# A convolution with max-pooling: whole copies of the second sum, and column maxima taken from SBUF

## The chip, the core and the metric

The kernel runs on one NeuronCore of a Trainium2 chip. Its engines work side by side, each through its own instructions in order: TensorE (PE in the profile) multiplies matrices into PSUM, VectorE (DVE), ScalarE (ACT) and GpSimd (POOL) do elementwise work, and SyncE (SP) issues DMAs, as ScalarE and GpSimd also may. PSUM has eight banks here, each of 128 partitions by 512 f32 numbers; GpSimd has no operand there in this kernel. The metric is the device time of one execution in microseconds. The median of three runs before the change is 103.07 us (103.0 to 103.2).

## The reference

```python
batch, c_in, h, w, c_out, k = 16, 64, 64, 64, 128, 3
x_pad = np.pad(x, ((0, 0), (0, 0), (pad, pad), (pad, pad)))
conv[b, co] += weight[co, ci, kh, kw] * x_pad[b, ci, kh:kh+h, kw:kw+w]   # over all ci, kh, kw
output[b, c, i, j] = np.max(conv[b, c, 2*i:2*i+2, 2*j:2*j+2])
```

It is a 3 x 3 convolution with padding, from 64 to 128 channels, on 16 images of 64 x 64, followed by the maximum over 2 x 2 blocks. Inputs and output are f32.

## The kernel before, in words

Two images lie in the 128 partitions together (64 channels each), as bf16 tiles `xb`. The output rows of a pair of images are cut into four quarters of 16 rows; there are 32 quarters `s`, and each has two halves `h`, one for each image. The two halves use different 64 rows of TensorE's array, so two chains of matmuls run side by side (`product` pairs them). One step of such a chain ("product") is three matmuls, one for each column of the filter, each of 512 or 504 columns. 512 columns are eight row pairs of 64 columns: one PSUM bank.

Of each pair of rows that is pooled, the kernel does not compute both rows in full. It makes two sums, a first one (bank `ta`) and a second one (bank `tb`), from products on combinations of image rows: `s` (the sum of the two rows), `e` (their difference) and `d` (the difference of rows two apart). In 52 of the 64 cases (type W) the first sum starts with P2 on `e`; `SE` copies it into the second bank as a seed (line L355); P0 adds to the first, P3 to the second; `EV` brings the negated first sum to SBUF (L349); `MX` writes the larger of the second sum and that back into the second bank (L360, VectorE, one input in PSUM and one in SBUF); P1 adds the product on `s`, and the second bank then holds the maximum over the two rows. In the other 12 (type K) the sums come from products straight on `xb` (PA, PB, PR) and `EV` does not negate (L345). The last quarter is worked off in two parts of half the rows; the second part (`s` = 32) keeps its two sums in two banks and has no row maximum.

What is left is the maximum over neighbouring columns. Before the change there are two ways: `OD` lets ScalarE copy the odd columns of the second bank to an SBUF tile `od` (L370, 256 of 512 columns), and `CM` lets VectorE take the maximum of the even columns in PSUM and of `od` (L389); or, where the order says `OD+`, nothing is copied and `CM` is a reduction from PSUM alone (L385). When both halves of a quarter are done, a DMA stores the tile `o` (L396). The part `s` = 32 has a reduction of its own over both banks, rows and columns at once (L378).

The combinations are made in SBUF: `S` on VectorE (L308), `E` on VectorE or, as `E+`, on GpSimd (L308), `D` on GpSimd or, as `D+`, on VectorE (L322); an `&` makes two quarters at once. A GpSimd instruction is told to wait for the VectorE instruction of this kind that stands last before it in the order: such VectorE instructions go through `on_vector`, which remembers them, and GpSimd's through `on_gpsimd`, which adds the wait (L66 to L72). Image loads (`L`) are issued by GpSimd under the same rule, except for the first rows, which SyncE loads as f32 and which are cast by ScalarE and VectorE (X steps).

At the start the weights are combined into blocks (g0, g1, g2, D0, D2, GS, GM, GP), transposed by TensorE (T steps, L146) and copied out of PSUM (V steps, L158 to L164).

The order of all steps is written out in one string, `ORDER`; each engine gets its own instructions in that order. `BANKS` is the list of PSUM banks, taken in turn by each new sum. A `+` sends a step to its other engine (VectorE for `SE+` and `EV+`).

Of the kernel before, what the change touches and what calls it, by code (L numbers as in the profile page):

```python
# [11 lines left out]
def kernel(  # L12
# [9 lines left out]
    nc = tc.nc  # L22
# [26 lines left out]
    o_pool = ctx.enter_context(tc.tile_pool(name="o_pool", bufs=12))  # L49
# [314 lines left out]
    def odd(s, h, alt):  # L364
        if alt:
            direct.add((s, h))
            return
        i0, i1 = span_of(s)
        dst = tile_of(od, od_pool, s, WO, "od")[:, h, i0:i1]
        nc.scalar.copy(out=dst, in_=acc[:, tb[s, h], i0:i1, 1::2])  # L370

    def colmax(s, h, free):
        i0, i1 = span_of(s)
        o = tile_of(ot, o_pool, s, WO, "o")
        t = acc[:, tb[s, h], i0:i1]
        if s == N:
            a, b = sorted((ta[s, h], tb[s, h]))
            nc.vector.tensor_reduce(  # L378
                out=o[:, h, i0:i1],
                in_=acc[:, a : b + 1 : b - a, i0:i1].rearrange("p k r (w two) -> p r w k two", two=2),  # L380
                axis=mybir.AxisListType.XY,
                op=MAX,
            )
        elif (s, h) in direct:
            nc.vector.tensor_reduce(  # L385
                out=o[:, h, i0:i1], in_=t.rearrange("p r (w two) -> p r w two", two=2), axis=mybir.AxisListType.X, op=MAX
            )
        else:
            nc.vector.tensor_tensor(out=o[:, h, i0:i1], in0=t[:, :, 0::2], in1=od[s][:, h, i0:i1], op=MAX)  # L389
        made.setdefault(s, []).append(h)  # L390
        if len(made[s]) < 2:
            return
# [44 lines left out]
    for m in ("G0", "G1", "G2"):  # L437
# [6 lines left out]
    ORDER = """  # L444
        g2+ g1 D2 g0 TG2 TD2 uG1+ XOa+ TG1 VD2+ VG2 D0 XOb+ GS+ XEa XEb+ X2 TD0 L.1.0.17 TG0 VD0 L.1.17.33
        VG0+ F.0.0 GP uGP+ F.2.0 F.0.1 F.3.1 GM F.1.0 S.0 X1+ F.1.1 EV+.0.1 EV.0.0 F.3.0 F.2.1 VG1+ uGM+
        PA1.1.0 PB1.1.0 L.0.49.64 PA2.1.0 MX.0.1 MX.0.0 PB2.1.0 PA1.1.1 PB1.1.1 PR.0.0 X4 PR.0.1 X3 L.1.33.64
        L.2.0.33 S.1 L.2.33.64 OD+.0.1 PA2.1.1 CM.0.1 EV.1.0 PB2.1.1 S.3 PB1.3.1 PA1.3.0 PB1.3.0 MX.1.0
        PA1.3.1 EV.1.1 OD.0.0 L.3.0.64 PA2.3.0 TGM MX.1.1 PR.1.1 PR.1.0 CM.0.0 PB2.3.1 PA2.3.1 S.2 OD.1.1
        PB2.3.0 D+.2 E&.2 CM.1.1 VGM EV.3.0 OD+.1.0 TGP P2.4.1 PA1.5.0 CM.1.0 MX.3.0 PA1.5.1 PB1.5.0 EV.3.1  # L450
        PA2.5.1 PA2.5.0 PR.3.0 SE.4.1 MX.3.1 D.4 VGP+ P0.4.1 PB2.5.0 P2.2.1 S.4 P3.4.1 EV.5.0 P2.4.0 PR.3.1
        S.5 E&.6 S&.7 EV.5.1 EV.4.1 OD.3.0 P2.6.0 SE.2.1 MX.5.0 L.4.0.64 CM.3.0 PR.5.0 SE.4.0 P0.2.1 P3.2.1
        OD.3.1 P0.4.0 P3.4.0 MX.4.1 EV.2.1 D.6 OD+.5.0 EV.4.0 CM.3.1 P2.6.1 PA1.9.0 SE.6.0 SE.6.1 CM.5.0 E+.8
        MX.2.1 MX.4.0 P1.4.1 P0.6.0 OD.4.1 P1.4.0 P1.2.1 P3.6.0 EV.6.0 S&.9 CM.4.1 D+.7 OD.2.1 P0.6.1 EV.6.1
        PB1.5.1 S.10 P3.6.1 P2.7.0 PA2.9.0 CM.2.1 MX.6.0 MX.6.1 P1.6.0 PB2.5.1 P2.7.1 D.10 OD.4.0 SE.7.0
        EV.9.0 MX.5.1 OD.6.0 P1.6.1 P0.7.0 P3.7.0 PR.5.1 P2.8.1 SE.7.1 EV.7.0 CM.4.0 CM.6.0 OD+.6.1 D.8 P2.8.0
        P0.7.1 CM.6.1 P3.7.1 PB1.9.0 MX.7.0 OD.5.1 CM.5.1 P1.7.0 SE.8.0 SE.8.1 E&.10 S.11 D+.11 P0.8.1 EV.7.1
        PB2.9.0 E&+.12 P0.8.0 OD.7.0 P3.8.0 EV.8.1 P2.10.1 P2.2.0 MX.7.1 EV.8.0 L.5.0.64 MX.9.0 PR.9.0 P3.8.1
        CM.7.0 MX.8.0 P1.8.0 P1.7.1 SE.10.1 P0.10.1 OD.7.1 P3.10.1 SE.2.0 P0.2.0 EV.10.1 MX.8.1 P2.11.0 CM.7.1
        P3.2.0 S&.12 P1.8.1 P2.10.0 MX.10.1 OD.8.0 OD.9.0 PA1.9.1 P1.10.1 CM.8.0 CM.9.0 D.14 PA1.15.1 OD.8.1  # L460
        EV.2.0 CM.8.1 SE.11.0 OD.10.1 SE.10.0 MX.2.0 PA2.9.1 P0.11.0 P1.2.0 CM.10.1 P0.10.0 P3.10.0 PB1.9.1
# [36 lines left out]
    BANKS = (
        "0123456710346520137365417346027351426507431270652347105234651370451275302641057631256401723451670312"
        "745632071634025674123706153427601526314"  # L500
# [9 lines left out]
    on_act = [i for i, v in enumerate(ORDER.split()) if v.split(".")[0] in ("EV", "SE", "OD")]  # L510
# [49 lines left out]
```

## Time and profile before

| what | value |
|---|---|
| median of the runs | 103.07 us |
| the profiled execution's own time | 103.78 us |
| its span, first to last instruction | 102.0 us |
| granted TensorE clock, mean | 0.999 |
| busy: PE / DVE / ACT / POOL | 95.7 / 91.2 / 82.3 / 56.7 us |
| L360, row maximum, VectorE, 512 columns | x62, 691 ns |
| L389, column maximum, VectorE, 256 from PSUM and `od` | x49, 415 ns |
| L385, column maximum as a reduction | x13, 682 ns |
| L370, copy of odd columns, ScalarE | x49, 379 ns |
| L355 and L349, whole copies, ScalarE | x50, 584 ns and x49, 603 ns |
| L322, `d` on GpSimd, 1024 columns bf16 | x18, 2129 ns |
| L308 and L322 on VectorE, 1024 columns bf16 | 681 ns |

An instruction's duration in the profile holds a fill and a drain that overlap with its neighbours: in a run of equal instructions they start closer together than they last. "Idle before" is the time an engine stood still ahead of an instruction, with what ended it.

### The profile page before, as it was taken

How to read it: one execution, taken by the hardware profiler on the slowest of the kernel's cores; microseconds unless marked ns; L12 is line 12 of the kernel's file. 1: busy time of each engine (PE TensorE's matmuls, PEld its weight loads, DVE VectorE, ACT ScalarE, POOL GpSimd, SP SyncE). 2: the span in 40 equal slices, each digit the busy share in tenths (PEclk: the TensorE clock that was granted, in tenths of full speed). 3: DMA queues.
4: the chain of work that ended last, by engine and by line, in shares of the span. 5: the costliest groups of instructions: out<-in, count | busy, mean ns of one | idle time of the engine just before them, and what ended most of it. 6: DMA issues, size and time to landing. Idle time of an engine off the chain costs nothing.

```text
span 102.0 us, 2471 instructions
## 1 busy us (share of the span) xinstructions
PE 95.7 (94%) x897; PEld 59.5 (58%) x897; DVE 91.2 (89%) x199; ACT 82.3 (81%) x182; POOL 56.7 (56%) x43
## 2 busy tenths in 40 slices
PE   6989999999999999999999999999999999999900
PEld 2468544565556664444676656776545777677800
DVE  3577999889999999999999989998999999999750
ACT  5467827899889899799967999998989998989410
POOL 2044427194693680953998666569688099930000
PEclk9999999999999999999999999999999999999999
DMA  2988999999999999999894379983260053220352
GB/s 75 263 322 175 162 171 214 225 235 231 228 218 245 327 202 191 240 209 212 143 330 151 116 146 190 202 284 105 70 231 14 16 195 107 103 103 0 135 202 86
DMA packets 11293, 18.04 MB, mean 177 GB/s; under 512 B 784, under 2 KB 9360, under 8 KB 10640
## 3 DMA queue, kind: packets, MB, share of 16 engines
q0 software_dynamic: 1584, 7.59, 40.8%
q1 hardware_dynamic: 9424, 10.16, 29.7%
q10 hardware_dynamic: 272, 0.13, 0.4%
q8 instruction: 7, 0.11, 0.4%
q14 instruction: 6, 0.05, 0.2%
HBM read 17.07 MB, written 8.39 MB: 250 GB/s over the span
## 4 chain that ended last, share of the span: by engine, by line
PE 88%; DMA 5%; DVE 1%; ACT 1%; SPq 0%; issue 0%; DVEq 0%
PE acc L197 88%; DMA kfirst<-in_x_dram 5%; DVE o L378 1%; PE acc L146 1%; ACT wt L162 0%; ACT xb L401 0%; SPq L81 0%; DVEq L555 0%
## 5 line engine op out<-in xcount | busy, mean ns | idle before, releaser
L197 PEld LDWEIGHTS <-wt 64*128 64x128 bf16 x864 | 56.2, 94 | 33.1 <-issue 4.2
L197 PE MATMUL acc<-d,wt 64*128 64x504 bf16 (+3 forms) x312 | 63.4, 373 | 0.0
L322 POOL TENSOR_TENSOR d<-xb 128x1024 bf16<-128x1024 bf16 x18 | 38.1, 2129 | 17.1 <-DVE s L308 9.0
L197 PE MATMUL acc<-s,wt 64*128 64x504 bf16 (+3 forms) x204 | 47.2, 367 | 0.0
L360 DVE TENSOR_TENSOR acc<-acc,ev 128x512 f32<-128x512 f32 (+1 forms) x64 | 42.1, 683 | 1.8 <-ACT od L370 0.4
L197 PE MATMUL acc<-e,wt 64*128 64x512 bf16 (+2 forms) x156 | 38.2, 372 | 0.0
L355 ACT COPY acc<-acc 128x512 f32<-128x512 f32 (+1 forms) x52 | 29.6, 576 | 3.5 <-PE acc L197 2.3
L349 ACT ACTIVATE ev<-acc 128x512 f32<-128x512 f32 (+1 forms) x51 | 29.9, 595 | 2.0 <-PE acc L197 1.3
L197 PE MATMUL acc<-xb,wt 64*128 64x504 bf16 (+6 forms) x192 | 27.2, 333 | 0.5 <-ACT wt L162 0.5
L370 ACT COPY od<-acc 128x256 f32<-128x256 f32 (+1 forms) x51 | 18.6, 374 | 5.2 <-PE acc L197 3.1
L389 DVE TENSOR_TENSOR o<-acc,od 128x256 f32<-128x256 f32 (+1 forms) x51 | 20.2, 410 | 0.9 <-ACT od L370 0.6
L308 POOL TENSOR_TENSOR e<-xb 128x512 bf16<-128x512 bf16 (+1 forms) x8 | 12.2, 1523 | 5.3 <-PE acc L197 2.7
L328 POOL DMA_DIRECT2D xb<-in_x_dram x11 | 6.2, 564 | 10.5 <-DVE xb L403 6.7
L308 DVE TENSOR_TENSOR s<-xb 128x1024 bf16<-128x1024 bf16 (+1 forms) x20 | 11.4, 575 | 0.2 <-ACT xb L401 0.2
L385 DVE TENSOR_REDUCE o<-acc 128x256 f32<-128x512 f32 x13 | 8.9, 682 | 0.2 <-PE acc L197 0.2
L345 ACT COPY ev<-acc 128x512 f32<-128x512 f32 x11 | 6.4, 588 | 0.9 <-PE acc L197 0.6
L308 DVE TENSOR_TENSOR e<-xb 128x1024 bf16<-128x1024 bf16 (+1 forms) x8 | 5.2, 649 | 0.0
L322 DVE TENSOR_TENSOR d<-xb 128x1024 bf16<-128x1024 bf16 (+1 forms) x8 | 5.2, 647 | 0.0
L506 PE MATMUL acc<-const-bfloat16-1.0 128*128 128x512 bf16 x8 | 3.6, 628 | 0.8 <-PEq L541 0.8
L146 PEld LDWEIGHTS <-wq 128*128 128x128 bf16 x25 | 2.2, 132 | 1.7 <-issue 0.8
L146 PE MATMUL acc<-ident,wq 128*128 128x128 bf16 x25 | 2.9, 291 | 0.0
L506 PEld LDWEIGHTS <-const-bfloat16-1.0 128*128 128x128 bf16 x8 | 1.0, 139 | 2.4 <-issue 2.4
(29 smaller groups left out, 18.0 us busy)
## 6 DMA issues: line engine op xcount, KB each, us to landing
out_dram<-o SPq DMA_DIRECT2D x31, 256.0 KB, 3.8
xb<-in_x_dram POOLq DMA_DIRECT2D x5, 1024.0 KB, 11.4
xb<-in_x_dram POOLq DMA_DIRECT2D x2, 496.0 KB, 10.5
xb<-in_x_dram POOLq DMA_DIRECT2D x1, 528.0 KB, 11.1
ksecond<-in_x_dram SPq DMA_DIRECT2D x1, 512.0 KB, 6.4
kthird<-in_x_dram SPq DMA_DIRECT2D x1, 512.0 KB, 7.1
wraw<-in_weight_dram SPq DMA_DIRECT2D x1, 288.0 KB, 2.9
kfirst<-in_x_dram SPq DMA_DIRECT2D x1, 288.0 KB, 4.7
```

Of the source, the lines that this page charges most:

```text
L146: nc.tensor.transpose(tp[:, (j - lo) * CO : (j - lo + 1) * CO], wq[:, j : j + 2, :].rearrange("a b c -> a (b c)"), ident,)
L197: nc.tensor.matmul(acc[:, t, i0:i1, o0:o1], wt[lo : lo + CI, tap_of(m0, kw, h), :], rows(lo, i0, i1, c0, c1), start=start and kw == 1, sto ...
L308: note(engine.tensor_tensor(out=dst, in0=in0, in1=in1, op=op))
L322: engine.tensor_tensor(out=row["d", s][:, 0:n, :], in0=t[:, f + 1 : f + 1 + n, :], in1=t[:, f - 1 : f - 1 + n, :], op=SUB)
L328: inst = on_gpsimd(nc.gpsimd.dma_start(out=xb[p][:, lo + 1 : hi + 1, :], in_=rows_of(p, lo, hi)))
L345: (nc.vector.tensor_copy if alt else nc.scalar.copy)(out=dst, in_=src)
L349: nc.scalar.mul(dst, src, -1.0)
L355: (nc.vector.tensor_copy if alt else nc.scalar.copy)(out=acc[:, t, i0:i1], in_=acc[:, ta[s, h], i0:i1])
L360: nc.vector.tensor_tensor(out=t, in0=t, in1=ev[s][:, h, i0:i1], op=MAX)
L370: nc.scalar.copy(out=dst, in_=acc[:, tb[s, h], i0:i1, 1::2])
L385: nc.vector.tensor_reduce(out=o[:, h, i0:i1], in_=t.rearrange("p r (w two) -> p r w two", two=2), axis=mybir.AxisListType.X, op=MAX)
L389: nc.vector.tensor_tensor(out=o[:, h, i0:i1], in0=t[:, :, 0::2], in1=od[s][:, h, i0:i1], op=MAX)
```

## The change

A new step `ODW` lets ScalarE copy all 512 columns of the second bank to SBUF, into an `od` tile that is twice as wide. `CM` then takes the maximum of the even and the odd columns of that tile: both of VectorE's inputs lie in SBUF. `CM&` does it for both halves of a quarter in one instruction of 512 columns. Counted in the order, 44 of the 64 cases use `ODW` (35 had `OD` before and 9 `OD+`), 17 `OD`, 3 `OD+`; 16 of the 44 go through the eight `CM&`. The pool of `o` tiles shrinks from 12 to 9. The order and the banks are written anew from start to end; among other things eight seeds and one eviction more are VectorE's (`SE+` eight times, `EV+` three times in place of two), five long `d` move from GpSimd to VectorE and four joint `e` the other way, and the transposes TG1 and TGM come before the first product.

```diff
-    o_pool = ctx.enter_context(tc.tile_pool(name="o_pool", bufs=12))
+    o_pool = ctx.enter_context(tc.tile_pool(name="o_pool", bufs=9))
...
-    def odd(s, h, alt):
+    whole = set()
+
+    def odd(s, h, alt, all_columns=False):
+        if all_columns:
+            whole.add((s, h))
+            nc.scalar.copy(out=tile_of(od, od_pool, s, W, "od")[:, h], in_=acc[:, tb[s, h]])
+            return
         if alt:
             direct.add((s, h))
             return
         i0, i1 = span_of(s)
-        dst = tile_of(od, od_pool, s, WO, "od")[:, h, i0:i1]
+        dst = tile_of(od, od_pool, s, W, "od")[:, h, i0:i1, 0:WO]
         nc.scalar.copy(out=dst, in_=acc[:, tb[s, h], i0:i1, 1::2])
 
-    def colmax(s, h, free):
+    def colmax(s, h, joint, free):
         i0, i1 = span_of(s)
         o = tile_of(ot, o_pool, s, WO, "o")
+        if joint:
+            assert {(s, 0), (s, 1)} <= whole
+            nc.vector.tensor_tensor(out=o, in0=od[s][:, :, :, 0::2], in1=od[s][:, :, :, 1::2], op=MAX)
+            store(s, free)
+            return
...
-        else:
-            nc.vector.tensor_tensor(out=o[:, h, i0:i1], in0=t[:, :, 0::2], in1=od[s][:, h, i0:i1], op=MAX)
+        elif (s, h) in whole:
+            t = od[s][:, h]
+            nc.vector.tensor_tensor(out=o[:, h], in0=t[:, :, 0::2], in1=t[:, :, 1::2], op=MAX)
+        else:
+            nc.vector.tensor_tensor(out=o[:, h, i0:i1], in0=t[:, :, 0::2], in1=od[s][:, h, i0:i1, 0:WO], op=MAX)
...
+        GS+ g2 g1 D2 GM TG2 D0 g0 uG1+ uGM+ TD2 L.1.0.17 VD2+ XOa+ XEa+ VG2+ L.1.17.33 XOb+ TG0 TD0 TG1 TGM
+        VG0+ VD0 VGM VG1+ X2 GP F.0.0 XEb L.0.49.64 S.0 X1+ uGP F.2.0 F.1.0 PA1.1.0 L.1.33.64 F.3.0 F.1.1
...
+        P2.19.1 P0.18.0 EV.17.0 S&.24 ODW.18.1 SE+.21.1 P3.18.0 EV.18.0 P2.20.0 CM&.13.1 ODW.16.1 MX.18.0
+        P2.22.0 P0.21.1 D.22 SE.19.1 EV.21.1 P3.21.1 MX.17.0 P0.19.1 P1.18.0 SE.22.0 P3.19.1 P1.17.0 S.23
...
-        CM.31.0 PA2.32.1 PRA.32.0 CM.29.1 P1.31.1 PA2.32.0 CM.32.1 CM.32.0 OD.31.1 CM.31.1
...
+        PB2.32.1 PB2.32.0 CM.30.0 OD.31.0 CM.31.0 MX.31.1 CM.32.1 PRB.32.0 P1.31.1 CM.32.0 OD.31.1 CM.31.1
```

More of the change, by code (lines that the diff above doesn't have):

```diff
@@ L387, in colmax, with store @@
             )
+        elif (s, h) in whole:
+            t = od[s][:, h]
+            nc.vector.tensor_tensor(out=o[:, h], in0=t[:, :, 0::2], in1=t[:, :, 1::2], op=MAX)
         else:
-            nc.vector.tensor_tensor(out=o[:, h, i0:i1], in0=t[:, :, 0::2], in1=od[s][:, h, i0:i1], op=MAX)
+            nc.vector.tensor_tensor(out=o[:, h, i0:i1], in0=t[:, :, 0::2], in1=od[s][:, h, i0:i1, 0:WO], op=MAX)
         made.setdefault(s, []).append(h)
-        if len(made[s]) < 2:
-            return
+        if len(made[s]) == 2:
+            store(s, free)
+    def store(s, free):
+        i0, i1 = span_of(s)
+        o = ot[s]
         p, q = place[quarter(s)]
@@ L444 @@
     ORDER = """
[L445 to L449, printed above, removed]
@@ new lines @@
+        PA2.1.1 OD+.0.0 X3 X4 PB2.1.0 PB2.1.1 PR.0.1 PA1.3.0 PB1.3.0 EV.1.1 EV.1.0 PA1.3.1 OD.0.1 L.2.33.64
+        CM.0.0 PB1.3.1 S.3 MX.1.1 MX.1.0 PR.1.0 CM.0.1 PA2.3.0 PB2.3.0 PA2.3.1 L.3.0.64 PB2.3.1 PR.1.1 EV.3.1
+        ODW.1.0 D+.2 E&.2 EV.3.0 P2.4.1 PA1.5.0 ODW.1.1 S&.4 MX.3.1 D.4 TGP SE.4.1 PR.3.1 PA1.5.1 PA2.5.0 VGP+
+        P0.4.1 EV.5.0 MX.3.0 CM&.1.1 P2.2.1 PR.3.0 OD+.3.1 CM.3.1 PB1.5.0 ODW.3.0 S.5 P2.4.0 E&.7 EV.4.1
+        SE.4.0 PA2.5.1 S&.7 D+.7 L.4.0.64 PB2.5.0 P3.4.1 SE.2.1 EV.5.1 MX.5.0 P0.2.1 P2.6.0 MX.4.1 SE.6.0
@@ new lines @@
+        P3.4.0 P3.2.1 P1.4.1 P0.4.0 D+.6 EV.2.1 PR.5.0 P0.6.0 CM.3.0 MX.2.1 E+.8 EV.4.0 P2.6.1 ODW.5.0 MX.4.0
+        D+.11 ODW.4.1 D+.8 P1.2.1 PA1.9.0 SE.6.1 P2.7.1 P3.6.0 P0.6.1 D.10 PA2.9.0 P1.4.0 EV.6.0 CM.5.0 OD.2.1
+        SE.7.1 CM.2.1 MX.6.0 CM.4.1 P3.6.1 EV.6.1 OD.4.0 P0.7.1 P2.7.0 CM.4.0 P1.6.0 P2.8.0 MX.6.1 PB1.5.1
+        S&.11 EV.9.0 SE.7.0 EV.7.1 L.5.0.64 P3.7.1 PB2.5.1 E&+.10 MX.7.1 P0.7.0 OD.6.0 P1.6.1 CM.6.0 MX.5.1
+        SE.8.0 P3.7.0 P0.8.0 P1.7.1 P2.8.1 EV.7.0 P3.8.0 PB1.9.0 OD.6.1 OD.7.1 MX.7.0 P1.7.0 EV.8.0 PR.5.1
@@ new lines @@
+        CM.6.1 SE.8.1 ODW.5.1 P2.10.1 CM.7.1 S&.8 ODW.7.0 SE.10.1 PB2.9.0 P2.2.0 P0.8.1 D+.12 MX.8.0 EV.8.1
+        P3.8.1 MX.9.0 E+.13 P0.10.1 P1.8.0 P3.10.1 SE.2.0 S&.15 PA1.9.1 PR.9.0 P0.2.0 S&.19 L.6.0.64 ODW.8.0
+        CM.5.1 EV.10.1 P2.11.0 PB1.9.1 MX.10.1 PA2.9.1 E+.14 OD.9.0 CM.9.0 P3.2.0 MX.8.1 EV.2.0 SE.11.0 MX.2.0
+        PB2.9.1 P2.10.0 EV.9.1 P0.11.0 E+.12 P1.2.0 MX.9.1 P1.8.1 SE.10.0 P0.10.0 EV.11.0 P1.10.1 PA1.15.0
+        ODW.8.1 D+.14 S&.12 E&.18 D+.13 PR.9.1 ODW.2.0 OD.9.1 EV.10.0 PA1.15.1 P3.11.0 P2.12.1 PA2.15.1
@@ new lines @@
+        ODW.10.1 PA2.15.0 P2.11.1 SE.12.1 P3.10.0 CM.9.1 EV.15.0 P2.12.0 CM.2.0 CM.10.1 MX.11.0 P0.12.1
+        P1.11.0 D.17 MX.10.0 P3.12.1 P1.10.0 P2.13.0 EV.15.1 E.17 S&.20 SE.11.1 EV.12.1 CM&.8.1 SE.12.0
+        MX.12.1 P0.12.0 P0.11.1 P3.11.1 ODW.11.0 P3.12.0 P2.14.1 ODW.10.0 EV.11.1 SE+.13.0 P1.12.1 D.18 E&+.22
+        EV.12.0 P2.13.1 P0.13.0 SE.14.1 P3.13.0 P2.14.0 P0.14.1 ODW.12.1 EV.13.0 EV.14.1 CM.7.0 CM.10.0
+        MX.11.1 P1.11.1 SE.13.1 MX.12.0 MX.13.0 S.22 D+.16 E.16 D+.19 P3.14.1 P1.12.0 P0.13.1 SE.14.0 P1.13.0
@@ new lines @@
+        P3.13.1 ODW.11.1 D.20 P0.14.0 P3.14.0 P2.17.1 PB1.15.1 EV.13.1 EV.14.0 ODW.13.0 ODW.12.0 MX.13.1
+        P1.13.1 MX.14.1 P1.14.1 PB1.15.0 PB2.15.0 PB2.15.1 P2.16.0 SE.17.1 ODW.13.1 MX.14.0 MX.15.0 ODW.14.1
+        P0.17.1 SE.16.0 D+.21 S&.16 P1.14.0 D.24 P3.17.1 E&+.21 L.7.0.64 MX.15.1 ODW.14.0 CM.12.0 PR.15.1
+        P2.18.1 PR.15.0 P2.19.0 D.23 SE+.19.0 EV.17.1 ODW.15.0 MX.17.1 P0.16.0 EV.16.0 P3.16.0 OD.15.1 MX.16.0
+        CM.15.1 CM&.14.1 SE.18.1 P0.19.0 P3.19.0 P2.16.1 P1.16.0 P1.17.1 EV.19.0 P2.17.0 SE.16.1 P0.18.1
@@ new lines @@
+        MX.19.0 OD.17.1 ODW.16.0 P0.16.1 CM&.11.0 CM.17.1 CM.12.1 P3.18.1 CM.15.0 EV.18.1 SE.17.0 P3.16.1
+        EV.16.1 P1.19.0 P2.21.1 P2.18.0 MX.18.1 P1.18.1 ODW.19.0 MX.16.1 P1.16.1 P0.17.0 SE.18.0 P3.17.0
+        P2.19.1 P0.18.0 EV.17.0 S&.24 ODW.18.1 SE+.21.1 P3.18.0 EV.18.0 P2.20.0 CM&.13.1 ODW.16.1 MX.18.0
+        P2.22.0 P0.21.1 D.22 SE.19.1 EV.21.1 P3.21.1 MX.17.0 P0.19.1 P1.18.0 SE.22.0 P3.19.1 P1.17.0 S.23
+        ODW.18.0 MX.21.1 P1.21.1 P0.22.0 CM.16.1 SE+.20.0 EV.19.1 ODW.17.0 CM.18.1 P3.22.0 MX.19.1 EV.22.0
@@ new lines @@
+        P2.22.1 ODW.21.1 P0.20.0 MX.22.0 P2.20.1 P1.19.1 P3.20.0 SE.22.1 P0.22.1 EV.20.0 ODW.19.1 SE+.20.1
+        P0.20.1 P1.22.0 P3.22.1 E&+.26 CM.18.0 P2.21.0 EV.22.1 P3.20.1 P2.23.0 CM.17.0 E&+.24 MX.20.0 CM.16.0
+        P1.20.0 ODW.22.0 SE.21.0 SE.23.0 P0.21.0 D.27 ODW.20.0 EV+.20.1 MX.22.1 MX.20.1 P3.21.0 P0.23.0
+        P2.24.1 P2.24.0 P1.22.1 P1.20.1 EV.21.0 SE.24.1 P3.23.0 ODW.22.1 D+.25 S&.27 P0.24.1 D.26 P2.25.1
+        MX.21.0 EV.23.0 ODW.20.1 P3.24.1 P1.21.0 SE+.24.0 CM&.22.1 EV.24.1 SE.25.1 MX.23.0 P0.24.0 P2.23.1
@@ new lines @@
+        CM.19.0 MX.24.1 P0.25.1 ODW.21.0 P3.25.1 EV.24.0 P3.24.0 SE.23.1 D.29 P0.23.1 P1.23.0 MX.24.0 P1.24.1
+        P2.25.0 P1.24.0 EV.25.1 ODW.23.0 CM.19.1 SE.25.0 P2.26.0 MX.25.1 P3.23.1 S&.29 OD.24.0 P0.25.0 P1.25.1
+        CM.24.0 P2.27.1 ODW.24.1 P2.26.1 EV.23.1 SE+.26.0 E&+.29 EV.25.0 MX.23.1 ODW.25.1 P1.23.1 P3.25.0
+        P0.26.0 P3.26.0 MX.25.0 CM.21.0 SE+.26.1 P1.25.0 SE.27.1 P2.27.0 P0.27.1 EV.26.0 E&+.31 D.28 MX.26.0
+        ODW.23.1 EV+.27.1 ODW.25.0 P1.26.0 P0.26.1 CM&.23.1 SE.27.0 CM.25.1 EV.26.1 P2.29.0 P3.26.1 D.30
@@ new lines @@
+        ODW.26.0 P2.28.1 P0.27.0 SE.29.0 MX.26.1 P3.27.1 SE.28.1 P1.26.1 P0.28.1 EV.27.0 CM.21.1 P3.28.1
+        P3.27.0 ODW.26.1 P0.29.0 EV.28.1 CM&.20.1 CM.25.0 MX.27.1 P1.27.1 P2.28.0 MX.27.0 EV.29.0 MX.28.1
+        P3.29.0 MX.29.0 S&.30 SE.28.0 P2.30.1 P1.28.1 P1.27.0 ODW.27.1 P0.28.0 OD+.28.1 P3.28.0 SE.30.1
+        EV.28.0 CM.28.1 P1.29.0 P2.29.1 MX.28.0 P0.30.1 P2.30.0 OD.27.0 CM.27.0 P1.28.0 SE.29.1 OD.29.0
+        EV.30.1 CM.29.0 P2.31.0 P3.30.1 P0.29.1 SE.30.0 P0.30.0 P3.30.0 D.31 CM.26.0 OD.28.0 MX.30.1 CM.28.0
@@ L500 @@
-        "745632071634025674123706153427601526314"
+        "0123456701235467302175647203162745132705634012765023654731054726103725136470251630754620153460732150"
+        "476135270134657124035764153246075126374"
     )
@@ L508 @@
         )
-    on_act = [i for i, v in enumerate(ORDER.split()) if v.split(".")[0] in ("EV", "SE", "OD")]
+    on_act = [i for i, v in enumerate(ORDER.split()) if v.split(".")[0] in ("EV", "SE", "OD", "ODW")]
     closing = [i for i, v in enumerate(ORDER.split()) if i > on_act[-1] and v.startswith("CM")]
@@ L516 @@
         alt, name = "+" in name, name.replace("+", "")
-        if name == "CM":
-            colmax(*args, free=len(closing) - closing.index(i) if i in closing else 0)
+        if name == "ODW":
+            odd(*args, False, True)
+        elif name == "CM":
+            colmax(*args, joint, free=len(closing) - closing.index(i) if i in closing else 0)
         elif name in joined:
```

51 lines of the change are left out of this document (4 added, 47 removed).

## The prediction

> **What bounds the kernel now.** I read the page's busy shares first, then the chain that ended last.
>
> ```profile
> PE 95.7 (94%) x897; PEld 59.5 (58%) x897; DVE 91.2 (89%) x199; ACT 82.3 (81%) x182; POOL 56.7 (56%) x43
> ...
> PE 88%; DMA 5%; DVE 1%; ACT 1%; SPq 0%; issue 0%; DVEq 0%
> ```
>
> In order of time, the same chain:
>
> ```profile
> 6.87 7.39 PE acc L197 x90
> 14.26 0.27 PE acc L146 x3
> 14.53 2.05 PE acc L197 x18
> 16.58 0.27 PE acc L146 x3
> 16.86 80.13 PE acc L197 x749
> 96.99 0.02 issue
> 97.01 1.29 DVE o L378 x2
> 98.30 0.20 DVEq L555
> ```
>
> TensorE is never released by anyone from 6.87 to 96.99 us, but for two groups of weight transposes. But it isn't alone. The table of stretches for 10 to 95 us:
>
> ```profile
> 10.00:95.00 85.00, 85.00 (x787) 52.15 (x785) 82.23 (x159) 75.55 (x167) 54.03 (x34) 1.00 0.73 175
> ```
>
> Of 85 us VectorE (third figure) is busy for 82.23 and has 2.77 idle; ScalarE (fourth) has 9.45; GpSimd (fifth) 30.97. VectorE is as good as full: a change here is paid in VectorE's time. What waits for the step that is changed, from the list of waits:
>
> ```profile
> PEld L197 <- DVE o L389: 0.4, 1, 0.4
> ...
> ACT acc L355 <- DVE o L389: 0.3, 1, 0.3
> ```
>
> All that TensorE and ScalarE lose to a PSUM bank that a column maximum still holds is 0.4 + 0.3 = 0.7 us.
>
> One more view, the timeline of VectorE and then of GpSimd from 47 to 56 us:
>
> ```profile
> 46.62 0.68 DVE L308 TENSOR_TENSOR e<-xb 128x1024 bf16<-128x1024 bf16 x1
> 47.33 0.42 DVE L389 TENSOR_TENSOR o<-acc,od 128x256 f32<-128x256 f32 x1
> 47.67 2.48 DVE L360 TENSOR_TENSOR acc<-acc,ev 128x512 f32<-128x512 f32 x4
> ...
> 55.78 0.41 DVE L389 TENSOR_TENSOR o<-acc,od 128x256 f32<-128x256 f32 x1
> 56.11 0.68 DVE L308 TENSOR_TENSOR s<-xb 128x1024 bf16<-128x1024 bf16 x1
> ```
>
> ```profile
> 47.45 2.13 POOL L308 TENSOR_TENSOR e<-xb 128x1024 bf16<-128x1024 bf16 x1 [2.72 <-PE acc L197]
> 49.53 6.30 POOL L322 TENSOR_TENSOR d<-xb 128x1024 bf16<-128x1024 bf16 x3
> ```
>
> While GpSimd works (47.45 to 55.83) VectorE runs only instructions with an operand in PSUM. Those with both inputs in SBUF (sums s, differences e, d) come before and after. That holds for the whole trace: of VectorE's 36 instructions on s, e and d none lies beside a GpSimd one by more than 0.13 us, though GpSimd is busy for 56% of the span. `on_gpsimd` makes each GpSimd step wait for the VectorE one listed before it (9.0 us of GpSimd's idle time before d is put down to `s`).
>
> **The change, part by part.** I take prices from start to start in an unbroken run, as the timeline gives them: VectorE 0.60 for 512 columns (four in 2.48 us, the last lasting 0.69) and 0.33 for 256; 0.60 for a reduction of 512 and for a bf16 sum of 1024; ScalarE 0.485 for 512 columns and 0.27 for 256; GpSimd 2.08 for 1024 and 1.11 for 512.
>
> ScalarE. 34 copies of odd columns go (-34 x 0.27 = -9.2), 44 whole copies come (I count 44 in the order, +21.3), 8 seeds go to VectorE (-3.9), one eviction too (-0.5): +7.7 us, in 9.45 us of idle time. 1.8 us are left: hidden, if nothing else delays it.
>
> VectorE. Column maxima against PSUM 49 to 15 (-11.3), direct reductions 13 to 3 (-6.0), 28 single maxima from SBUF (+9.3), 8 joint ones for both halves (+4.8), 8 seeds (+4.8), one eviction (+0.6), sums and differences 26 to 28 long and 10 to 8 short ones (+0.5): **+2.7 us**, against 2.77 idle. No row shows an f32 maximum of two stepped SBUF inputs. Lower end: the bf16 sums of the same 0.33 and 0.60. Upper end: the f32 sum of weights with a step of nine (192 columns, 0.41 start to start, so about 0.55 for 256), +9.5 us in all. I take the lower: ScalarE's copies of every second column show no extra for a step of two (0.27 for 256 against 0.485 for 512).
>
> GpSimd. d 18 to 13 and a short one, e 3 to 7 long, 5 to 4 short: -2.1 us, off the path.
>
> Banks. A whole copy frees the bank when ScalarE ends, not when VectorE does: at most the 0.7 us above. The changed bank order and the output buffers (12 to 9) I cost at nothing: stores land in 3.8 us at the median, while nine quarters are some 23 us of work.
>
> Start. TG1 and TGM move ahead of the first product: 22 transposes, 0.107 each (19 took 2.21 us before, the last one's 0.3 with them), from 4.23: the first product at about 6.6 instead of 6.87 (-0.27), if the eviction of D2, now ahead of ScalarE's first cast, is done by then; it is (g2, g1, g0 and two short copies from 3.63 end near 5.5). The 0.27 of transposes at 14.26 goes as well; that only hands slack to VectorE. GpSimd's loads are issued behind weight steps that end about 1 us earlier.
>
> End. Before, both L378 reductions wait for TensorE's end, and L389 for both (97.01 to 98.50). After, CM.32.1 stands ahead of the last products and ScalarE's last copy no longer waits for VectorE: one reduction of 0.6 less, -0.6.
>
> Where the new maxima lie. They are the first VectorE instructions with two SBUF inputs beside GpSimd. They are not marked `on_vector`, so no GpSimd step waits for them, and the order puts them between the PSUM steps that fill GpSimd's time. An example: after S&.24 the VectorE order has SE+.21.1 (0.60), CM&.13.1 (0.60), MX, MX, S.23, and GpSimd does D.22 (2.08) right behind S&.24. CM&.13.1 starts at 0.60, when D.22 still has 1.48 to go. By such counting 31 of the 36 have GpSimd beside them, for 12.0 of their 14.1 us. The trace has no such case, so the price has two ends. Below: 0 (62 row maxima with one SBUF input run beside GpSimd at 0.69 as ever). Above: each waits for the running GpSimd step. Counting along every run, the first such waits are 0.88 (D.4), 1.05 (D.10), 1.75 (D.17), 0.78 (D.18), 1.48 (D.24), 1.48 (D.22), 1.48 (E.26), 0.88 (D.26), 0.18 (E.29): 10.0 us; with the later ones in the same runs 20.4. I take the first waits, since the rows it is nearest to are those of s, e and d, which draw two inputs from SBUF at as many bytes per microsecond (1024 bf16 or 512 f32 columns in 0.60) and are kept apart from GpSimd. GpSimd starts later than its VectorE release alone would have it: 7.6 us of idle before its sums is put down to PE or to itself, against 50 busy, about 15%. So 10.0 less 15% = **8.5 us**. MX, seeds and evictions queue behind such a wait on VectorE, and TensorE waits for the banks that they free.
>
> The Trainium skill (SBUF — State Buffer, Who interferes with whom) says that a VectorE instruction with two SBUF inputs contends with a GpSimd one that reads SBUF, and that whoever issues first holds the shared pair for the whole instruction. No run here shows it yet; the trace agrees so far that such pairs never meet. By that rule alone the price would be the upper end, 20.4 us.
>
> **The sum.** The profiled execution took 103.78 us around its span of 102.0; the median of the runs is 103.07, so I add differences to the median. With VectorE as the bound: +2.7 work, -2.77 idle, -0.65 for its wait at the end (which holds the -0.6 of the end), -0.3 start, +8.5 waits: +7.5, so **110.5 us**.
>
> **Rivals.**
> 1. No price for the meeting, and VectorE keeps full (faster). +2.7 - 2.77 - 0.65 - 0.3 + what VectorE still idles. The bank freed early lets VectorE put column maxima off, so it may idle for as little as 0.4: 102.4 us. It decides below 1.0 us of idle. For it: no row shows that the meeting costs. Against: ScalarE is left 1.8 us, TensorE 1 or 2, VectorE nothing, and three full queues in order seldom fit.
> 2. No price for the meeting, but VectorE idles as before. +2.7 - 0.6 - 0.3 = +1.8: 104.9 us; if stepped f32 reads cost the upper end, up to 114.
> 3. Full waits at each meeting. +20.4 in place of 8.5: 122.4 us. Against: GpSimd also waits when VectorE comes first, and has 31 us of idle time.
>
> **How the numbers follow.** Some price for the meeting (the forecast and rival 3): 0.56, of which rival 3 has 0.14. Rival 1: 0.28, of which 0.05 fall within 0.2%; rival 2: 0.16. Faster 0.23, same 0.05, slower 0.72; 0.2% is about what a measurement of this kernel can tell from no change. The forecast's own range, price 2 to 17 us, is 104 to 119. The whole range leaves out the best tenth of rival 1 and the last of rival 3: 102.0 to 121.
>
> **What will show it.** The group of new maxima (o<-od): a mean of some 0.41 for single ones and idle time or length beyond it wherever GpSimd runs; GpSimd steps beyond 2.13 would show that VectorE came first. TensorE's waits for ScalarE's seeds and for L360 should grow to several us in the stretch from 50 to 90. If the maxima last 0.41 beside GpSimd and VectorE is busy for over 98% from 10 us to the end, rival 1 or 2 holds and the forecast is wrong by its largest term. A first product at 6.6 and a single reduction behind TensorE's end would confirm the start and the end.

## The result and the profile after

The changed kernel takes 124.4 us (median of four runs, 123.97 to 125.2); the kernel before took 103.13 us beside it (103.0 to 103.25). The ratio is 1.207, with a 95% interval of 1.200 to 1.214: slower by 21.3 us. The forecast was 110.5 us in a range of 102.0 to 121.0. The sign is right and the time lies 3.4 us above the range; rival 3 (122.4 us) came nearest. The profiled execution took 124.11 us around a span of 122.2. Executions over 1.5% longer than the fastest of their kernel, at a lower granted clock, are left out of the ratios and ranges below.

Busy shares, and the chain that ended last, from the page of the changed kernel:

```profile
PE 101.9 (83%) x897; PEld 55.2 (45%) x897; DVE 113.5 (93%) x200; ACT 90.2 (74%) x182; POOL 57.4 (47%) x43
...
PE 23%; DVE 20%; issue 11%; ACT 5%; DVEq 0%; ACTq 0%
```

Before, TensorE alone was 88% of the chain; now the chain hops between TensorE and VectorE. VectorE's busy time has grown by 22.3 us (91.2 to 113.5) with one instruction more. The groups of VectorE, different shapes kept apart, say where:

```profile
L360 DVE TENSOR_TENSOR acc<-acc,ev 128x512 f32<-128x512 f32 x62 | 40.7, 687 | 1.6 <-PE acc L197 1.4
L401 DVE TENSOR_TENSOR o<-od 128x256 f32<-128x256 f32 x28 | 25.8, 940 | 0.0
L383 DVE TENSOR_TENSOR o<-od 128x512 f32<-128x512 f32 x8 | 11.6, 1454 | 0.0
...
L403 DVE TENSOR_TENSOR o<-acc,od 128x256 f32<-128x256 f32 x15 | 6.1, 412 | 0.0
```

The last line is the old way, one input in PSUM: 412 ns, as before. The new single maxima (L401) have the same 256 columns and last 940 ns on average; the joint ones (L383) have the 512 columns of the row maximum (L360, 687 ns) and last 1454. The idle time in front of them is 0.0. Taking 0.413 and 0.680 as their length without company (the undisturbed ones in this trace), 28 x 0.527 + 8 x 0.774 = 20.9 us are too much. What they are spent on shows beside GpSimd. VectorE around the example of the prediction, CM&.13.1 (the line L383), and GpSimd's D.22 below it:

```profile
72.41 0.68 DVE L355 COPY acc<-acc 128x512 f32<-128x512 f32 x1
73.01 2.29 DVE L383 TENSOR_TENSOR o<-od 128x512 f32<-128x512 f32 x1
75.23 1.28 DVE L360 TENSOR_TENSOR acc<-acc,ev 128x512 f32<-128x512 f32 x2
```

```profile
72.63 2.12 POOL L322 TENSOR_TENSOR d<-xb 128x1024 bf16<-128x1024 bf16 x1 [4.70 <-PE acc L197]
```

The maximum begins at 73.01, when GpSimd has 1.74 us of its own step left, and ends 0.55 us after GpSimd does. It lasts 1.61 us too long; the prediction counted 1.48 for this one. The two row maxima behind it queue. A second place has both orders of arrival. VectorE from 46.7 us, then GpSimd:

```profile
46.70 0.68 DVE L383 TENSOR_TENSOR o<-od 128x512 f32<-128x512 f32 x1
...
48.50 3.40 DVE L401 TENSOR_TENSOR o<-od 128x256 f32<-128x256 f32 x2
```

```profile
46.92 2.44 POOL L322 TENSOR_TENSOR d<-xb 128x1024 bf16<-128x1024 bf16 x1 [2.90 <-PE acc L197]
49.32 2.29 POOL L308 TENSOR_TENSOR e<-xb 128x1024 bf16<-128x1024 bf16 x1
```

The joint maximum was there first, keeps its 0.68, and GpSimd's d takes 2.44 instead of 2.13. The two single maxima at 48.50 come second: together 3.40 us instead of 0.75. The first waits for the end of D.18; by then GpSimd goes on with E&+.22 at 49.32, and the second waits 1.92 us more for that. In all, 16 of the 36 new maxima are longer than alone, by 0.13 to 2.48 us, 21.0 us together. Each of the 16 ends 0.27 to 0.29 us (256 columns) or 0.54 to 0.56 us (512 columns) behind the end of a GpSimd step. GpSimd loses little: d x13 at 2255 and e x7 at 2225 ns against 2129 before, 2.3 us in all.

The longest maximum, CM&.14.1, does not fit the order of arrival. VectorE, then GpSimd:

```profile
65.33 3.16 DVE L383 TENSOR_TENSOR o<-od 128x512 f32<-128x512 f32 x1
```

```profile
65.20 0.57 POOL L328 DMA_DIRECT2D xb<-in_x_dram  x1
65.79 2.13 POOL L322 TENSOR_TENSOR d<-xb 128x1024 bf16<-128x1024 bf16 x1
```

It begins 0.46 us ahead of GpSimd's d, while GpSimd issues a load of image rows, and yet it waits for the whole d, which loses nothing. Two more runs below have one such maximum each, begun beside the issue of a load with a GpSimd step right behind (3.89 us long in the old order, 3.17 with the marks). In the old order one that began beside an issue with no step right behind, at 75.12 us, kept its 0.41. So the recorded start does not always tell who comes first; why was not tested.

What the others wait for, from the list of waits:

```profile
PEld L197 <- issue: 26.8, 42, 2.7
POOL d L322 <- PE acc L197: 17.4, 5, 4.7
PE acc L197 <- DVE acc L360: 12.2, 8, 2.3
ACT od L369 <- PE acc L197: 9.7, 9, 1.8
```

TensorE waits 12.2 us for row maxima, which queue behind the long column maxima; before, no such wait was among its large ones. ScalarE and GpSimd then wait for TensorE. The table of stretches (length, then PE, PEld, DVE, ACT and POOL busy, granted clock, DMA share, GB/s) adds one thing:

```profile
10.00:50.00 40.00, 37.68 (x338) 19.91 (x334) 39.97 (x68) 34.06 (x69) 19.72 (x16) 1.00 0.97 219
50.00:60.00 10.00, 7.75 (x58) 4.81 (x56) 8.56 (x13) 6.02 (x12) 3.74 (x2) 0.83 0.16 54
```

VectorE has 0.03 us left in 40. From 50 to 60 us, where TensorE's gaps are long, the granted clock is 0.83 on average; before the change it was 1.00 from the first product to the last.

### The profile page after: what moved, and what is told of

Read it like the earlier page. It is cut to its first block, busy times and chain, and to the rows that moved or that the text cites. A ratio compares the mean times of both kernels' runs of the same rounds, so it can differ in the third digit from the quotient of the medians.

```text
span 122.2 us, 2479 instructions
## 1 busy us (share of the span) xinstructions
PE 101.9 (83%) x897; PEld 55.2 (45%) x897; DVE 113.5 (93%) x200; ACT 90.2 (74%) x182; POOL 57.4 (47%) x43
## 4 chain that ended last, share of the span: by engine, by line
PE 23%; DVE 20%; issue 11%; ACT 5%; DVEq 0%; ACTq 0%
PE acc L197 23%; DVE acc L360 9%; DVE o L401 5%; DVE acc L355 2%; ACT acc L355 2%; ACT ev L349 2%; ACT od L369 1%; DVE ev L347 1%; DVE o L389 1%; DVE o L383 1%; ACT od L376 1%; DVE o L403 1%; DVE s L308 1%; DVEq L575 0%; DVE d L322 0%
## 5 line engine op out<-in xcount | busy, mean ns | idle before, releaser
L197 PE MATMUL acc<-d,wt 64*128 64x504 bf16 (+3 forms) x312 | 69.9, 389 | 2.2 <-DVE acc L355 2.2
L197 PE MATMUL acc<-s,wt 64*128 64x504 bf16 (+3 forms) x204 | 47.8, 375 | 12.3 <-DVE acc L360 12.2
L322 POOL TENSOR_TENSOR d<-xb 128x1024 bf16<-128x1024 bf16 (+1 forms) x14 | 30.4, 2176 | 30.6 <-PE acc L197 17.4
L360 DVE TENSOR_TENSOR acc<-acc,ev 128x512 f32<-128x512 f32 (+1 forms) x64 | 41.5, 678 | 1.6 <-PE acc L197 1.4
L369 ACT COPY od<-acc 128x512 f32<-128x512 f32 x44 | 25.6, 593 | 10.0 <-PE acc L197 9.7
L197 PE MATMUL acc<-xb,wt 64*128 64x504 bf16 (+7 forms) x192 | 27.1, 333 | 0.0
L401 DVE TENSOR_TENSOR o<-od 128x256 f32<-128x256 f32 x28 | 25.8, 940 | 0.0
L308 POOL TENSOR_TENSOR e<-xb 128x1024 bf16<-128x1024 bf16 (+1 forms) x11 | 20.2, 1848 | 7.6 <-DVE s L308 5.3
L383 DVE TENSOR_TENSOR o<-od 128x512 f32<-128x512 f32 x8 | 11.6, 1454 | 0.0
L308 DVE TENSOR_TENSOR s<-xb 128x1024 bf16<-128x1024 bf16 (+1 forms) x19 | 11.4, 605 | 0.1
L376 ACT COPY od<-acc 128x256 f32<-128x256 f32 (+1 forms) x17 | 6.2, 365 | 3.3 <-PE acc L197 3.1
L322 DVE TENSOR_TENSOR d<-xb 128x1024 bf16<-128x1024 bf16 x12 | 8.0, 677 | 0.0
L403 DVE TENSOR_TENSOR o<-acc,od 128x256 f32<-128x256 f32 (+1 forms) x17 | 6.6, 396 | 0.0
```

The source lines that it names most:

```text
L197: nc.tensor.matmul(acc[:, t, i0:i1, o0:o1], wt[lo : lo + CI, tap_of(m0, kw, h), :], rows(lo, i0, i1, c0, c1), start=start and kw == 1, sto ...
L308: note(engine.tensor_tensor(out=dst, in0=in0, in1=in1, op=op))
L322: engine.tensor_tensor(out=row["d", s][:, 0:n, :], in0=t[:, f + 1 : f + 1 + n, :], in1=t[:, f - 1 : f - 1 + n, :], op=SUB)
L360: nc.vector.tensor_tensor(out=t, in0=t, in1=ev[s][:, h, i0:i1], op=MAX)
L369: nc.scalar.copy(out=tile_of(od, od_pool, s, W, "od")[:, h], in_=acc[:, tb[s, h]])
L383: nc.vector.tensor_tensor(out=o, in0=od[s][:, :, :, 0::2], in1=od[s][:, :, :, 1::2], op=MAX)
```

## The experiments

Two theories. The forecast's kind: the new maxima have to wait for GpSimd, since both their inputs come from SBUF. The rival: the order, the banks, ScalarE's extra work or the reads of every second column cost the time, and the lengths beside GpSimd are something else.

### GpSimd without reads, in the changed kernel and in the one before

```diff
-        note(engine.tensor_tensor(out=dst, in0=in0, in1=in1, op=op))
+        if on_pool:
+            note(engine.memset(dst, 0.0))
+            return
+        note(engine.tensor_tensor(out=dst, in0=in0, in1=in1, op=op))
```

The same is done for d.

> The changed kernel, but GpSimd fills its d and e tiles with zeros in place of computing them from the image rows (so 25 of the differences are left out and the output is not the convolution): GpSimd reads nothing from SBUF. Theory (VectorE's two-input maxima wait for GpSimd instructions that read SBUF): every o<-od maximum lasts 0.41 (256 columns) or 0.68 (512 columns), and the time falls by about the 21 us of their waits, to 101 to 105 us. Rival A (an f32 maximum of two stepped SBUF inputs is slow by itself): the mean of 0.94 and 1.45 stays, and so do 124 us. Rival B (the new order, its banks or three full queues cost the time): the maxima get short, but the time stays above 115 us.

> The kernel before with the same edit (26 differences on GpSimd left out and filled with zeros): the control for e1. Theory: 103 us, within 1 us, since nothing waits for GpSimd there. If it falls by several us, e1 has to be read against it and not against 103.

The changed kernel falls to **102.2 us** (101.58 to 102.8), ratio 0.990 (0.984 to 0.995) to the kernel before: 22 us are gone. The control takes 103.24 us, ratio 0.999 (0.996 to 1.002): in the old kernel GpSimd's reads, and its speed, cost nothing. Groups of the changed kernel with a GpSimd that only writes:

```profile
L407 DVE TENSOR_TENSOR o<-od 128x256 f32<-128x256 f32 x28 | 11.2, 418 | 0.0
...
L389 DVE TENSOR_TENSOR o<-od 128x512 f32<-128x512 f32 x8 | 5.5, 683 | 0.0
```

The same 36 maxima last 418 and 683 ns; the longest single one 426. So reading every second f32 number from SBUF has no price of its own, and an instruction of GpSimd that writes alone doesn't hold them up. The stretch of 10 to 95 us of that run:

```profile
10.00:95.00 85.00, 84.97 (x809) 56.22 (x805) 84.48 (x164) 80.02 (x166) 24.76 (x32) 1.00 0.70 174
```

TensorE is full again, and VectorE has 0.52 idle instead of 2.77. This is rival 1 as the prediction wrote it (102.4 us, 0.4 idle). GpSimd's step is also shorter here (0.95 instead of 2.13 us). But ten of the 36 maxima begin while one runs, with 0.24 to 0.84 us of it left, and none is longer than alone, so the shorter step does not explain it.

### The same work with one input

```diff
-            nc.vector.tensor_tensor(out=o[:, h], in0=t[:, :, 0::2], in1=t[:, :, 1::2], op=MAX)
+            nc.vector.tensor_reduce(
+                out=o[:, h], in_=t.rearrange("p r (w two) -> p r w two", two=2), axis=mybir.AxisListType.X, op=MAX
+            )
```

The joint maximum is changed in the same way; GpSimd does its full work.

> The changed kernel, but the 36 maxima from SBUF are reductions over neighbouring columns of the same od tile: one SBUF input instead of two, twice the columns read. Theory (only the second SBUF input meets GpSimd): each lasts 0.68 (512 columns read) or about 1.2 (1024 read) whether GpSimd runs or not; VectorE gets 28 x 0.27 + 8 x 0.53 = 11.8 us more work and loses 20.9 us of waits: about 115 us, 111 to 117. Rival (any SBUF reading of VectorE meets GpSimd): lengths scatter up to 2.3 us as now and the time is above 124 us.

Measured: **111.93 us** (111.68 to 112.28), ratio 1.084 (1.081 to 1.088). Its groups and the stretch of 10 to 95 us:

```profile
L405 DVE TENSOR_REDUCE o<-od 128x256 f32<-128x512 f32 x28 | 18.3, 672 | 0.0
...
L383 DVE TENSOR_REDUCE o<-od 128x512 f32<-128x1024 f32 x8 | 9.6, 1203 | 0.0
```

```profile
10.00:95.00 85.00, 80.52 (x699) 42.87 (x697) 85.00 (x144) 75.06 (x148) 50.58 (x31) 1.00 0.68 163
```

A reduction goes over twice as many numbers and is longer by itself: 28 x 0.26 + 8 x 0.52 = 11.4 us of VectorE's work more than maxima without company. It still saves 12.5 us, since it never waits: 672 ns is the length of a reduction from PSUM (682), and GpSimd's d is back at 2127. VectorE is busy for 85.00 of 85 us, so its work is the time: 102.2 + 11.4 = 113.6, against 111.93. It is the second input from SBUF that meets GpSimd's reads; the read of SBUF as such does not. That the instruction is of another kind doesn't matter: the row maxima (L360) are a `tensor_tensor` with one SBUF input, and they last 687 ns in the changed kernel.

### The changed order with even columns from PSUM

```diff
-            t = od[s][:, h]
-            nc.vector.tensor_tensor(out=o[:, h], in0=t[:, :, 0::2], in1=t[:, :, 1::2], op=MAX)
+            nc.vector.tensor_tensor(out=o[:, h], in0=t[:, :, 0::2], in1=od[s][:, h, :, 1::2], op=MAX)
```

The joint maxima become two such instructions.

> The changed kernel with its order, banks and whole copies, but each of the 44 maxima takes the even columns from PSUM and only the odd ones from the copy; the eight joint ones become two each (+0.5 us in all). One SBUF input per instruction; the bank is held until VectorE is done. Theory: maxima of 0.41, no waits for GpSimd, and banks held as before the change: 102 to 106 us. Rival B (order and banks cost the time): above 115 us. Rival C (the early release of the bank is worth much): above 108 us with TensorE waiting for o.

Measured: 119.73 us, ratio 1.160 (1.157 to 1.163). It misses its expectation and does not say what it was meant to. In the new order many column maxima stand behind the next use of their bank; there they read the next sum, so the even columns are not those of the sum that they belong to, and they wait for that sum. The 28 single ones:

```profile
L403 DVE TENSOR_TENSOR o<-acc,od 128x256 f32<-128x256 f32 x28 | 11.5, 419 | 8.6 <-PE acc L197 5.1 <-ACT ev L349 1.9 <-ACT acc L355 1.4
```

They last 419 ns and don't wait within themselves, but 8.6 us ahead of themselves. What the run suggests is that the new order lives on the bank that the whole copy frees; it says nothing for or against the order with SBUF maxima.

### The parts in the old order

One kernel takes before's order and banks and does only the whole copies (the even columns still come from PSUM); the other also takes the maxima from SBUF. Both have 9 output tiles instead of 12, as the changed kernel has.

```diff
-        dst = tile_of(od, od_pool, s, WO, "od")[:, h, i0:i1]
-        nc.scalar.copy(out=dst, in_=acc[:, tb[s, h], i0:i1, 1::2])
+        dst = tile_of(od, od_pool, s, W, "od")[:, h, i0:i1]
+        nc.scalar.copy(out=dst, in_=acc[:, tb[s, h], i0:i1])
...
-            nc.vector.tensor_tensor(out=o[:, h, i0:i1], in0=t[:, :, 0::2], in1=od[s][:, h, i0:i1], op=MAX)
+            c = od[s][:, h, i0:i1]
+            nc.vector.tensor_tensor(out=o[:, h, i0:i1], in0=c[:, :, 0::2], in1=c[:, :, 1::2], op=MAX)
```

> The kernel before with its order; ScalarE copies whole banks (51 x 0.215 = about 10.5 us more on ScalarE, 9.45 idle there), but the maximum takes its even columns from PSUM as before and its odd ones from the copy. It prices ScalarE's part alone. Theory: 103.5 to 107 us, maxima at 0.41.

> The kernel before, with its order and banks, but each of the 51 copies of odd columns is a whole copy and the maximum takes both inputs from it (9 output tiles): the edit alone, without the new order. Theory: the old order puts these maxima into GpSimd's time as it did those from PSUM; counted along its runs the waits are 24.6 us (against 0.4 for the old maxima), so 125 to 130 us with ScalarE's extra 10.5 us partly hidden. Rival B (the new order is what costs): close to 105 us.

Copies alone: **108.82 us**, ratio 1.049 (1.044 to 1.054). That is above the expectation. In the old order ScalarE's extra 0.21 us per copy is not hidden, though ScalarE has 5.86 us of 85 idle: the maximum stands close behind its copy in the order and waits for it. From the list of waits of that kernel:

```profile
DVE o L389 <- ACT od L370: 4.1, 13, 0.6
```

With SBUF maxima as well: **131.5 us**, ratio 1.269 (1.264 to 1.274), a little above the expectation. Its group of maxima:

```profile
L390 DVE TENSOR_TENSOR o<-od 128x256 f32<-128x256 f32 x49 | 49.5, 1024 | 1.4 <-ACT od L370 1.1
```

49 x (1.024 - 0.413) = 29.9 us of waits; the times of the two kernels differ by 22.7. So the maxima from SBUF are slow in the old order too, by more (49 of them, where the changed kernel has 36 for 44 halves): the rewriting of the order is not the cause.

### Keeping the two apart

First, every new maximum is marked, single and joint, so that GpSimd's next step waits for it.

```diff
-            nc.vector.tensor_tensor(out=o[:, h], in0=t[:, :, 0::2], in1=t[:, :, 1::2], op=MAX)
+            on_vector(nc.vector.tensor_tensor(out=o[:, h], in0=t[:, :, 0::2], in1=t[:, :, 1::2], op=MAX))
```

> The changed kernel, but the maxima from SBUF are marked like the other VectorE instructions with two SBUF inputs, so that a GpSimd step waits for those listed before it. The order is the same. Theory: maxima listed ahead of a GpSimd step no longer meet it, but the step ends later, and the sums and differences behind it meet it instead: part of the 21 us moves to s, d and e on VectorE; 110 to 120 us. If the wait alone mends it, 105 us or less.

Measured: **121.4 us** (121.0 and 121.82), ratio 1.173 (1.165 to 1.180), against 1.207 without the marks. That is above the expectation: some 3 us are won. The groups are from an execution of 124.25 us:

```profile
L401 DVE TENSOR_TENSOR o<-od 128x256 f32<-128x256 f32 x28 | 23.2, 846 | 0.0
...
L383 DVE TENSOR_TENSOR o<-od 128x512 f32<-128x512 f32 x8 | 10.2, 1280 | 0.0
```

The maxima are still 28 x 0.433 + 8 x 0.600 = 16.9 us too long, 4.0 us less than without the marks. Some 1.5 us come back on VectorE's own e and d, as expected: the two e of 512 columns last 914 ns instead of 410, the twelve long d 714 instead of 677. A mark keeps GpSimd from starting ahead of the maxima listed before it; it does nothing for the ones listed behind, which VectorE comes to while GpSimd works.

Second, the marks, and each of these maxima that the order has ahead of VectorE's last s is moved down to just ahead of VectorE's next s, e or d, where GpSimd stands still anyway. In the example of the prediction (parts of the order):

```diff
-S&.24 ODW.18.1 SE+.21.1 P3.18.0 EV.18.0 P2.20.0 CM&.13.1 ODW.16.1 MX.18.0
+S&.24 ODW.18.1 SE+.21.1 P3.18.0 EV.18.0 P2.20.0 ODW.16.1 MX.18.0
...
 P2.22.0 P0.21.1 D.22 SE.19.1 EV.21.1 P3.21.1 MX.17.0 P0.19.1
-P1.18.0 SE.22.0 P3.19.1 P1.17.0 S.23
+P1.18.0 SE.22.0 P3.19.1 P1.17.0 CM&.13.1 S.23
```

> As e6, and every maximum from SBUF before the last sum is moved down the order to just before the next VectorE sum or difference, so that all VectorE work with two SBUF inputs stands together and GpSimd's time holds only work on PSUM. Theory: the new maxima last 0.41 or 0.68 at most places; but GpSimd's time is no longer filled: counted along the runs VectorE lacks 6.7 us of PSUM work there and waits for it at the first maximum or sum. So the time falls by about 14 us, to 108 to 113 us. Rival (the waits have nothing to do with GpSimd): 124 us.

Measured: **112.0 us** (111.58 to 112.04), ratio 1.080 (1.076 to 1.085). Groups, and the stretch of 10 to 95 us:

```profile
L401 DVE TENSOR_TENSOR o<-od 128x256 f32<-128x256 f32 x28 | 11.4, 443 | 0.0
...
L383 DVE TENSOR_TENSOR o<-od 128x512 f32<-128x512 f32 x8 | 6.2, 782 | 0.0
```

```profile
10.00:95.00 85.00, 79.47 (x714) 44.16 (x710) 77.78 (x141) 75.12 (x151) 50.57 (x31) 1.00 0.63 152
```

The same instructions with the same operands, elsewhere in time: 443 and 782 ns, so 1.7 us of the 20.9 are left, and 12.4 us of the time are won. But VectorE now idles for 7.2 us of 85, as the expectation has it (6.7): its work with two SBUF inputs stands in a bunch while GpSimd stands still, and the work that could go beside GpSimd is not there in time. How the 9.8 us above 102.2 divide between VectorE, TensorE and the later GpSimd steps was not taken apart.

### The two small gains of the new end and start, in the old kernel

At the end, banks 4 and 5, and 1 and 2, are exchanged throughout, so that ScalarE's last copy no longer waits for VectorE. Then the changed kernel's start is put ahead of that:

```diff
-        g2+ g1 D2 g0 TG2 TD2 uG1+ XOa+ TG1 VD2+ VG2 D0 XOb+ GS+ XEa XEb+ X2 TD0 L.1.0.17 TG0 VD0 L.1.17.33
+        GS+ g2 g1 D2 GM TG2 D0 g0 uG1+ uGM+ TD2 L.1.0.17 VD2+ XOa+ XEa+ VG2+
...
```

> The kernel before with two pairs of banks renamed throughout (4 with 5, 1 with 2): the two banks of each last reduction lie side by side, so that no other bank lies between them. Theory: one of the two last reductions no longer waits for TensorE's end and ScalarE's last copy no longer waits for the reductions, as in the changed kernel: 0.6 us less, 102.5 us. Rival: the end is hidden by the stores: 103.1 us.

> As b1, and the start is that of the changed kernel: the blocks g1 and GM are transposed ahead of the first product, g2 is cast by ScalarE, the eviction of D2 comes ahead of the first image cast. The changed kernel's first product started at 6.26 instead of 6.87 us. Theory: 0.6 us at the start and up to 0.3 for three transposes that leave the middle, if VectorE follows: 101.6 to 102.2 us. Rival (VectorE is the bound and starts no earlier): as b1, 102.5 us.

The banks alone: 103.1 us against 103.34, ratio 0.996 (0.994 to 0.999). With the start as well: **102.78 us**, ratio 0.995 (0.992 to 0.999), the fastest kernel here that computes the whole convolution, by half a percent. Both gains are smaller than expected. The first product of the second kernel starts at 6.60 us, but the chain of its profiled execution, in order of time, then has this:

```profile
9.52 7.26 DMA xb<-in_x_dram
...
16.83 5.36 PE acc L197 x48
```

A load of image rows ends at 16.79, and TensorE, started earlier, comes to it 0.53 us too early; there the gain at the start is waited away. This execution is the longest of the twelve (103.71 us; they begin at 102.33), and whether the others wait as much was not looked at.

## Why the prediction was wrong

**What bounds the kernel** held: VectorE was as good as full, and what the change added to VectorE's time came out as time, 20.9 us of waits in 21.3 us of loss.

**The step that failed** is the price of the meeting: "I take the first waits", and then "10.0 less 15% = **8.5 us**". The measured value is 20.9 us. Where a maximum met a running GpSimd step, it waited for the whole rest of the step, and it did so every time, not only the first time in a run. Both corrections downward were wrong.

- Only the first waits. The later ones, 20.4 - 10.0 = 10.4 us by the count, measured 10.6. The reason that I gave, that the nearest rows are those of s, e and d and are kept apart from GpSimd, says nothing of whether a second maximum waits. Where GpSimd has two steps behind the same VectorE sum, both listed ahead of the maxima (D.18 and E&+.22 behind S&.20), the second starts at once, and the next maximum meets that one.
- The 15% for late starts of GpSimd. The nine first waits, 10.0 us by the count, measured 10.4; singly, CM&.13.1 1.61 (1.48 counted), CM.7.0 behind D.18 0.73 (0.78), the maximum beside D.17 1.87 (1.75), and the one beside E&+.29 nothing (0.18).

Counted in full along the order, the same list gave 20.4 us: the count was the better instrument than the guess about it. That it comes so close holds some luck, since 2.48 of the 20.9 us are CM&.14.1, which began ahead of the step that it waited for.

By the Trainium skill (SBUF — State Buffer, Who interferes with whom) whoever issues first holds the shared pair for the whole instruction. The trace agrees: VectorE second, 2.29 us instead of 0.68; VectorE first, GpSimd 2.44 instead of 2.13; CM&.14.1, first by its recorded start and yet second, is the exception. The page also says that a GpSimd instruction that only writes doesn't contend with two SBUF inputs, and that a VectorE instruction with one SBUF input, outside its two-port modes, doesn't contend with GpSimd: here 418 ns and 672 ns, without a wait. I had the rule with its price, 20.4 us, and gave it 0.14; my objection was that GpSimd also waits when VectorE comes first. It waited for 2.3 us in all. A likely reason is their lengths: a GpSimd step of 2.1 us is more often under way when a maximum starts than a maximum of 0.4 us when a step starts.

**The range** ended at 121 for that reason: rival 3, whose own time was 122.4, lay beyond it.

**VectorE's work without waits.** The price of a maximum, 0.33 start to start and no extra for the step of two, is right (0.41 alone; 418 ns with a GpSimd that only writes). The sum of +2.7 can't be read off directly: busy time grew by 1.2 us (91.2 to 92.4 in that run), which also holds the drain in front of each gap and so is not the same measure. The term is not settled closer than these 1.5 us.

**ScalarE** (+7.7 in 9.45 idle, hidden) is right for the new order, where TensorE was busy for 84.97 of 85 us once GpSimd only wrote. It is not a matter of the sum alone: in the old order the same kind of copies cost 5.3 us, with idle time to spare.

**The banks and the buffers** cost nothing, also by that run; the bank freed early is, as the run with even columns from PSUM suggests, what lets the maxima be put off.

**The start** gained more than its -0.27. First product of the changed kernel, 6.26 instead of 6.87 (I had 6.6, counted from 4.23, where the trace has the first transpose at 4.19). The old kernel with this start has 6.60; here the last six transposes stand 0.055 us apart instead of 0.107:

```profile
6.26 4.02 PE L197 MATMUL acc<-xb,wt 64*128 64x256 bf16 x60
```

**The end** came as described: one reduction behind TensorE's end at 117.83.

```profile
117.26 1.29 DVE L389 TENSOR_REDUCE o<-acc 128x128 f32<-128x512 f32 x2
118.47 0.28 DVE L403 TENSOR_TENSOR o<-acc,od 128x128 f32<-128x128 f32 x1
```

Neither shows in the total. **Rival 1**, a time of 102.4 us if the meeting were free, is what the kernel does when it is free (102.2): everything about the change but the meeting is worth 1%, if GpSimd's shorter steps gain nothing here, as they gained nothing in the old kernel. Adding 20.9 to 102.2 gives 123.1; the last 1.3 us to 124.4 were not traced to one cause. The stretches with the granted clock at 0.83 are one candidate.

## What to carry to other kernels

Before a VectorE operand is moved from PSUM to SBUF, count the VectorE instructions that would then have two SBUF inputs, and see where GpSimd reads SBUF at that time; the price here was the whole rest of GpSimd's step at each meeting, so a count along the order gave it (20.4 us for 20.9), and no discount was due. If GpSimd can't be kept apart, a form with one SBUF input can be cheaper although it is longer by itself (111.9 against 124.4 us here). An engine at 93% busy with no idle time in front of it may still be waiting: compare the mean length of a group with its shortest member or with the same shape elsewhere.

## What the runs showed of the hardware that was not expected

- The wait lies inside VectorE's recorded duration. 20.9 us of it appear nowhere in the list of waits and as 0.0 us of idle time; only the length of the instruction tells (a joint maximum of 0.68 us alone lasted up to 3.16).
- A wait that is told to GpSimd in the program mends only one of the two orders of arrival: 16.9 us of too long maxima were left of 20.9.
- f32 maxima with both inputs in SBUF, every second number, take the same time as those with one input in PSUM: 418 and 417 ns for 256 columns in the run where GpSimd only writes.
- The granted clock fell to 0.5 for 3.41 us at a time in the changed kernel (53.55 to 56.96 us and 104.75 to 108.16); it was 1.00 elsewhere while TensorE worked. In the 3.41 us ahead of these TensorE was busy for 1.16 and 1.53. But from 67.20 to 70.61 it was busy for 1.46, and the clock stayed at 1.00; what the gap has to be is open.
